# Both feed-forward blocks by column blocks with twelve of 22 up pairs each as seven half-size products, and the last four down tiles by halves of the tokens

## The chip, the cores and the metric

The kernel runs on one core of a Trainium2 chip. The metric is the device time of one execution in microseconds. TensorE (PE) multiplies, VectorE (DVE) and ScalarE (ACT) do the elementwise work, and SyncE (SP) issues the transfers between HBM and SBUF. Matrix products land in eight PSUM banks.

## The reference

A trunk of two layers on 512 tokens of width 1024, in float32. Every layer adds a token mixer and then a feed-forward block to the residual stream:

```python
for i in range(2):                       # mixer 0: gated linear attention, mixer 1: short gated convolution
    x = x + mixer_i(rmsnorm(x, norm_mix_g[i]))
    h = rmsnorm(x, norm_ffn_g[i])
    up = causal_dwconv(h @ w_up[i], conv_w[i])       # 1024 -> 2 * 2816, three taps along the tokens
    a, u = up[..., :2816], up[..., 2816:]
    x = x + (silu(a) * u) @ w_down[i]                # 2816 -> 1024
return rmsnorm(x, final_norm_g)
```

## The kernel before

Activations lie channel by token: the residual is eight tiles `x[k]` of 128 channels by 512 tokens. Every float32 operand is split into two parts of a shorter type, h and l (`halve` for weights, `split_to` and `norm_parts` for activations), and one product is three matmuls (`mm3`: wh xh, wh xl, wl xh) that accumulate in a PSUM bank. The split of a weight unit is a cast on ACT (L124) and a subtraction on DVE (L125).

`Weights` holds the order of all weight units. A raw unit is loaded by SP into one of six buffers (`wraw`), split into one of four pairs of buffers (`wsp`), and handed out by `take`, which at each call has a unit split that is used two calls later.

The feed-forward block has 22 pairs `j`: an a tile and a u tile of 128 channels. A plain pair is two `group`s of 24 matmuls (eight k, three each, 512 tokens wide). Each result is scaled by `r`, convolved (`conv3`: one ACT and two DVE operations), joined with Silu, and split into `g{j}`. A down tile `dn{m}` is a sum over the `g{j}`.

In layer 0 `ffn_blocks` goes by `BLOCKS` of 6, 5, 5 and 6 pairs: while it makes the pairs of one block it also makes the eight down tiles over the block before, one or two after each pair, and adds each to `x[m]`. The last block's eight tiles stand at the end. `SEVEN` names nine pairs that are made by Strassen's scheme: the two output tiles, the two halves of k and the two halves of the tokens form a 2 by 2 product, done as seven products of 12 matmuls, 256 tokens wide. `seven_first` does four of them (`updc`, `upab`), a down tile follows, and `seven_last` does three. Sums of weights are made on DVE by `Weights.forms` (L134 to L141), sums of activations once for each layer by `seven_forms` after pairs 1 to 4, and the results are put together by `L634` to `L651`.

In layer 1 `ffn_up` makes 22 plain pairs, and then eight down tiles follow over all 22 pairs at once (`DOWN_CUTS` cuts their weights in three). The eighth, `dn7`, is done by halves of the tokens (`last_group`, `last_square`), so that the final norm of the first half (`last_sums`, `last_rms`, `last_rows`, `last_out`) lies beside the matmuls of the second. What remains after the last matmul is the residual, square, sum, root, broadcast, scaling and output of the second half.

The order of instructions on each engine is not the program's order alone: a planner takes the program's dependencies and its own costs and places an instruction as soon as it finds it ready, earlier program lines first.

Of the kernel before, what the change touches and what calls it, by code (L numbers as in the profile page):

```python
# [15 lines left out]
P = 128  # L16
# [9 lines left out]
EPS = 1e-6  # L26
UNIT = 1024
WARM = 10
DOWN_CUTS = ((0, 8), (8, 16), (16, 22))
BLOCKS = ((0, 6), (6, 11), (11, 16), (16, 22))  # L30
SEVEN = (7, 9, 10, 12, 14, 15, 17, 19, 21)


@with_exitstack
def trunk_kernel(ctx, tc, xT, w_qk, w_v, w_g, w_up_gate, b_gate, w_go, w_sc, w_so, w_up, w_dn,
# [15 lines left out]
    def wk(name, shape=(P, T), dt=F32, bufs=2, tag=None, pool=work):  # L51
        return pool.tile(list(shape), dt, tag=tag or name, name=name, bufs=bufs)


    def tk(name, shape, bufs=2):
        return wk(name, shape, bufs=bufs, pool=tiny)

    def bt(tag, name, shape=(P, T), dt=F32):
        return big.tile(list(shape), dt, tag=tag, name=name)
# [135 lines left out]
    def ff_steps():  # L195
        steps = [("up", j) for j in range(*BLOCKS[0])]
        for b in range(1, len(BLOCKS)):
            n = BLOCKS[b][1] - BLOCKS[b][0]
            for i, j in enumerate(range(*BLOCKS[b])):
                dn = [("dn", b - 1, m) for m in range(KD * i // n, KD * (i + 1) // n)]  # L200
                steps += [("s1", j), dn[0], ("s2", j)] + dn[1:] if j in SEVEN else [("up", j)] + dn
        return steps + [("dn", len(BLOCKS) - 1, m) for m in range(KD)]

    for st in ff_steps():
        if st[0] == "dn":
            a, b = BLOCKS[st[1]]
            W.add(w_dn[0, st[2]][:, a * P:b * P])
        elif st[0] == "s1":
            pair = W.add_pair(w_up[0, 2 * st[1]], w_up[0, 2 * st[1] + 1])
        elif st[0] == "s2":  # L210
            W.end_pair(pair)
        else:
            W.add(w_up[0, 2 * st[1]])
            W.add(w_up[0, 2 * st[1] + 1])
    for src in ([w_sc[i] for i in range(3 * KD)] + [w_so[i] for i in range(KD)]
                + [w_up[1, j] for j in range(2 * NFF)]
                + [w_dn[1, m][:, a * P:b * P] for m in range(KD) for a, b in DOWN_CUTS]):
        W.add(src)
    take = W.take


# [53 lines left out]
    def group(name, xs, nunits=1):  # L275
        out = ps(name)
        k = 0
        for _ in range(nunits):
            for w in take():
                mm3(out, w, xs[k], k == 0, k == len(xs) - 1)  # L280
                k += 1
        assert k == len(xs)
        return out
# [28 lines left out]
    def sum_parts(sq):  # L312
        h = wk("sh", dt=F32R, tag="sq")
        l = wk("sl", dt=F32R, tag="sq")
        S.copy(h, sq)
        V.tensor_sub(l, sq, h.bitcast(F32))
        return h, l

    def inv_rms_rows(parts, cnt):

        o = ps("sums")
        for i, a in enumerate(parts):
            PE.matmul(o, lhsT=onesr, rhs=a, start=i == 0, stop=i == 1)
        r = wk("r", bufs=2)
        S.activation(r, o, AF.Sqrt, bias=epst, scale=1.0 / cnt)  # L325
        V.reciprocal(r, r)  # L326
        return r
# [243 lines left out]
    residual(lambda m: go[m] if m < 2 else group(f"go{m}", yparts), 1)  # L571


    def ffn_up(l):
        gp, r = [], None
        for j in range(NFF):
            ups = [group("up0", xparts)]
            if j == 0:
                sums = sum_parts(acc[0])
            ups.append(group("up1", xparts))  # L580
            if j == 0:
                r = inv_rms_rows(sums, D)
            cs = []
            for i in range(2):
                u = wk("u", bufs=3)
                V.tensor_mul(u, ups[i], r)  # L586
                cs.append(conv3(u, ffcw[:, l, i * NFF + j, :], f"c{i}"))
            S.activation(cs[0], cs[0], AF.Silu)  # L588
            V.tensor_mul(cs[1], cs[1], cs[0])
            gp.append(split_to(cs[1], f"g{j}", f"b{j}"))  # L590
        return gp

    def seven_forms(k, gi, y):


        lo, hi = slice(0, HT), slice(HT, T)
        g1, g2 = col(gi, k), col(gi, k + 4)
        S.activation(y[:, lo], x[k][:, hi], AF.Copy, scale=g1)
        S.activation(y[:, hi], x[k + 4][:, hi], AF.Copy, scale=g2)
        ta, tb = wk("ta", tag="sq"), wk("tb", tag="sq")  # L600
        V.scalar_tensor_tensor(ta[:, lo], x[k][:, lo], g1, y[:, lo], op0=ALU.mult, op1=ALU.subtract)
        V.tensor_sub(tb[:, lo], y[:, lo], y[:, hi])
        V.scalar_tensor_tensor(ta[:, hi], x[k][:, lo], neg[:, k:k + 1], tb[:, lo], op0=ALU.mult, op1=ALU.add)
        V.scalar_tensor_tensor(tb[:, hi], x[k + 4][:, lo], g2, ta[:, hi], op0=ALU.mult, op1=ALU.add)
        a = split_to(ta, f"ta{k}", f"b{14 + 2 * k}")
        b = split_to(tb, f"tb{k}", f"b{15 + 2 * k}")
        return [tuple(p[:, c] for p in t) for t in (a, b) for c in (lo, hi)]
# [45 lines left out]

    def ffn_blocks(l, gi, gnext):
        gp, r, tf = {}, None, [[], [], [], []]
        V.tensor_scalar_mul(neg, vec[:, gi * KD:(gi + 1) * KD], -1.0)
        for st in ff_steps():
            if st[0] == "dn":
                _, b, m = st
                part = group(f"dn{m}", [gp[j] for j in range(*BLOCKS[b])])  # L660
                V.tensor_add(x[m], x[m], part)  # L661
                if b == len(BLOCKS) - 1:
                    norm_parts(m, gnext)
                    norm_squares(m)
                continue
            j = st[1]
            if st[0] == "s1":
                begun = seven_first(tf)
                continue
            if st[0] == "s2":  # L670
                us = seven_last(*begun, tf)
                for u in us:
                    V.tensor_mul(u, u, r)  # L673
            else:
                ups = [group("up0", xparts)]
                if j == 0:
                    sums = sum_parts(acc[0])
                ups.append(group("up1", xparts))
                if j == 0:
                    r = inv_rms_rows(sums, D)  # L680
                    y = wk("y", tag="acc", bufs=1)
                us = [wk("u", bufs=3) for _ in range(2)]
                for u, up in zip(us, ups):
                    V.tensor_mul(u, up, r)
            cs = [conv3(us[i], ffcw[:, l, i * NFF + j, :], f"c{i}") for i in range(2)]
            S.activation(cs[0], cs[0], AF.Silu)  # L686
            V.tensor_mul(cs[1], cs[1], cs[0])
            gp[j] = split_to(cs[1], f"g{j}", f"b{j % 11}")
            if len(SEVEN) and 1 <= j <= 4:
                for t, f in zip(tf, seven_forms(j - 1, gi, y)):  # L690
                    t.append(f)

    HT = T // 2
    neg = tk("neg", (P, KD), bufs=1)
    ffn_blocks(0, 1, 2)


# [18 lines left out]
    residual(lambda m: group(f"so{m}", yparts), 3)  # L716


    gp = ffn_up(1)
    for i in range(3):  # L720
        W.hold[len(W.units) - 3 + i] = lambda i=i: [
            [bt(f"x{2 * i + j}{hl}", f"wlast{i}{j}{hl}", (P, T), F32R) for hl in "hl"] for j in range(2)]
    for m in range(KD - 1):
        V.tensor_add(x[m], x[m], group(f"dn{m}", gp, nunits=3))  # L724
        norm_squares(m)
    wlast = take() + take() + take()

    def last_group(op, th, ks):
        c = slice(th * HT, (th + 1) * HT)
        for k in ks:  # L730
            gh, gl = gp[k]
            mm3(op, wlast[k], (gh[:, c], gl[:, c]), k == 0, k == NFF - 1)

    def last_square(op, th):
        c = slice(th * HT, (th + 1) * HT)
        V.tensor_add(x[KD - 1][:, c], x[KD - 1][:, c], op)
        sq = wk("sq", (P, HT))
        V.tensor_mul(sq, x[KD - 1][:, c], x[KD - 1][:, c])
        return sq

    def last_sums(pt, sq, th):
# [31 lines left out]
            V.tensor_tensor(o, o, rb.unsqueeze(1).to_broadcast([P, 2, HT]), ALU.mult)  # L773
            nc.sync.dma_start(out[a:a + 2, :, c].rearrange("a p t -> p a t"), o)

    ops = [ps("dn7a")[:, 0:HT], ps("dn7b")[:, 0:HT]]
    pts = [[ps(f"sums{th}{t}") for t in range(2)] for th in range(2)]
    last_group(ops[0], 0, range(NFF))
    last_scale(0, range(KD - 1))
    sq = last_square(ops[0], 0)  # L780
    last_scale(0, (KD - 1,))
    last_group(ops[1], 1, range(0, 5))
    last_sums(pts[0], None, 0)
    last_sums(pts[0], sq, 0)
    rl = last_rms(pts[0], 0)
    last_scale(1, range(KD - 1))
    last_group(ops[1], 1, range(5, 10))
    rb = last_rows(rl)
    last_out(rb, 0)
    last_group(ops[1], 1, range(10, NFF - 1))  # L790
    last_sums(pts[1], None, 1)
    last_group(ops[1], 1, (NFF - 1,))
    sq = last_square(ops[1], 1)
    last_scale(1, (KD - 1,))
    last_sums(pts[1], sq, 1)
    last_out(last_rows(last_rms(pts[1], 1)), 1)
# [53 lines left out]
```

## Time and profile before

| | before |
|---|---|
| time, median of 3 runs | 1111.91 us (1111.66 to 1113.05) |
| profiled execution: time / span | 1112.06 us / 1110.0 us |
| PE busy | 1100.6 us, 99% |
| DVE busy | 754.6 us, 68% |
| ACT busy | 488.9 us, 44% |
| mean granted clock of TensorE | 0.997 |

The span is from the first to the last instruction of the profiled execution. The 2.06 us beside it lie around it. Matmuls are pipelined, so one lasts longer than the distance to the next; the pace is read from the chain of work, which gives a stretch and the number of its matmuls.

### The profile page before, as it was taken

To read this page: it belongs to the slowest core of one execution; us is meant where nothing else is said; L and a number is where in the kernel's file an instruction comes from. 1 tells how busy PE (TensorE), PEld (TensorE's weight loads), DVE (VectorE), ACT (ScalarE), POOL (GpSimd) and SP (SyncE) were. 2 spreads that over 40 slices of the span, in tenths; PEclk is the share of its full clock that TensorE was granted. 3 is DMA by queue.
4 is the path that set the end of the run, shared out by engine and by line. 5 is a ranking of instruction groups with operands and counts; after the bars stand their busy time and mean duration, and the time that the engine had idled before them with its cause. 6 is when DMAs were issued, how large, how long until landed. Compare 5 with 4: busy or idle time off the path is not lost.

```text
span 1110.0 us, 13420 instructions
## 1 busy us (share of the span) xinstructions
PE 1100.6 (99%) x5344; PEld 931.3 (84%) x5344; DVE 754.6 (68%) x1019; ACT 488.9 (44%) x688; POOL 5.1 (0%) x18
## 2 busy tenths in 40 slices
PE   9999999999999999999999999999999999999997
PEld 7888888888889889888888888888888888888887
DVE  7864675599787888887866555558777777743313
ACT  6565664465344444444543222335444444432321
POOL 1000000000000000000000000000000000000000
PEclk9999999999999999999999999999999999999998
DMA  8222123323233233333332233322222233333302
GB/s 297 96 94 77 62 72 114 96 71 105 85 101 98 90 97 113 103 98 83 119 113 95 95 98 96 106 99 96 95 95 95 95 95 96 88 102 88 102 1 77
DMA packets 34338, 108.19 MB, mean 97 GB/s; under 512 B 3746, under 2 KB 6562, under 8 KB 34276
## 3 DMA queue, kind: packets, MB, share of 16 engines
q1 hardware_dynamic: 34276, 107.34, 30.2%
q8 instruction: 42, 0.69, 0.2%
q14 instruction: 20, 0.16, 0.0%
HBM read 105.23 MB, written 2.10 MB: 97 GB/s over the span
## 4 chain that ended last, share of the span: by engine, by line
PE 99%; DMA 0%; DVE 0%; ACT 0%; SPq 0%; issue 0%; DVEq 0%
PE up L273 34%; PE dn L273 20%; PE updc L614 5%; PE g L273 4%; PE v L273 4%; PE scb L273 4%; PE scu L273 4%; PE scc L273 4%; PE go L273 4%; PE so L273 4%; PE upab L614 4%; PE k L273 2%; PE q L273 2%; PE dn7b L273 1%; PE dn7a L273 1%; PE o L494 1%
## 5 line engine op out<-in xcount | busy, mean ns | idle before, releaser
L124 ACT CAST wh<-wr 128x1024 fp32r<-128x1024 f32 (+4 forms) x227 | 217.0, 957 | 356.1 <-issue 88.3
L125 DVE TENSOR_TENSOR wl<-wr,wh 128x1024 fp32r<-128x1024 f32 (+4 forms) x227 | 250.4, 1106 | 107.8 <-ACT wh L124 106.3
L273 PE MATMUL up<-xh,wh 128*128 128x512 f32 x560 | 217.9, 389 | 0.0
L273 PE MATMUL up<-xl,wh 128*128 128x512 f32 x560 | 217.9, 389 | 0.0
L273 PE MATMUL up<-xh,wl 128*128 128x512 f32 x560 | 217.8, 389 | 0.0
L273 PEld LDWEIGHTS up<-xl,wh 128*128 128x128 f32 x560 | 105.1, 188 | 21.8
L273 PEld LDWEIGHTS up<-xh,wh 128*128 128x128 f32 x560 | 105.1, 188 | 21.8
L273 PEld LDWEIGHTS up<-xh,wl 128*128 128x128 f32 x560 | 105.1, 188 | 21.6
L332 ACT ACTIVATE c<-u,ffcw 128x512 f32<-128x512 f32 x88 | 62.1, 720 | 19.2 <-DVE u L673 11.8
L334 DVE SCALAR_TENSOR_TENSOR c<-u,ffcw,c 128x510 f32<-128x510 f32 x88 | 64.9, 747 | 1.7
L333 DVE SCALAR_TENSOR_TENSOR c<-u,ffcw,c 128x511 f32<-128x511 f32 x88 | 64.7, 746 | 1.2 <-ACT c L332 0.6
L586 DVE TENSOR_TENSOR u<-up,r 128x512 f32<-128x512 f32 x44 | 30.1, 688 | 37.7 <-PE up L273 37.6
L588 ACT ACTIVATE c<-c 128x512 f32<-128x512 f32 x22 | 13.9, 632 | 41.5 <-DVE c L334 41.4
L661 DVE TENSOR_TENSOR x<-x,dn 128x512 f32<-128x512 f32 x32 | 21.9, 684 | 13.8 <-PE dn L273 13.5
L326 DVE RECIPROCAL r<-r 128x512 f32<-128x512 f32 x8 | 26.8, 3352 | 6.3 <-ACT r L325 6.3
L309 ACT ACTIVATE sq<-x 128x512 f32<-128x512 f32 x34 | 21.0, 623 | 19.0 <-DVE x L724 17.8
L686 ACT ACTIVATE c<-c 128x512 f32<-128x512 f32 x22 | 13.9, 631 | 26.6 <-DVE c L334 26.5
L273 PE MATMUL g<-xh,wh 128*128 128x512 f32 x64 | 25.6, 400 | 0.0
L273 PE MATMUL v<-wh,xh 128*128 128x512 f32 x64 | 25.3, 395 | 0.0
L273 PE MATMUL g<-xh,wl 128*128 128x512 f32 x64 | 24.9, 390 | 0.0
L273 PE MATMUL v<-wh,xl 128*128 128x512 f32 x64 | 24.9, 390 | 0.0
L273 PE MATMUL v<-wl,xh 128*128 128x512 f32 x64 | 24.9, 389 | 0.0
(924 smaller groups left out, 2384.8 us busy)
## 6 DMA issues: line engine op xcount, KB each, us to landing
wr<-in_w_up SPq DMA_DIRECT2D x88, 512.0 KB, 3.4
wr<-in_w_sc SPq DMA_DIRECT2D x24, 512.0 KB, 3.4
wr<-in_w_dn SPq DMA_DIRECT2D x24, 384.0 KB, 3.1
wr<-in_w_dn SPq DMA_DIRECT2D x16, 512.0 KB, 3.5
wr<-in_w_dn SPq DMA_DIRECT2D x16, 320.0 KB, 2.9
wr<-in_w_v SPq DMA_DIRECT2D x8, 512.0 KB, 3.6
wr<-in_w_g SPq DMA_DIRECT2D x8, 512.0 KB, 3.5
wr<-in_w_go SPq DMA_DIRECT2D x8, 512.0 KB, 3.4
```

The lines of the kernel that those rows point to most:

```text
L124: S.copy(hh, src)
L125: V.tensor_sub(ll, src, hh.bitcast(F32))
L273: PE.matmul(out, lhsT=a, rhs=b, start=first and i == 0, stop=last and i == 2)
L309: S.activation(sq, x[k], AF.Square)
L326: V.reciprocal(r, r)
L332: S.activation(c, u, AF.Copy, scale=cw[:, 2:3])
L333: V.scalar_tensor_tensor(c[:, 1:], u[:, :T - 1], cw[:, 1:2], c[:, 1:], op0=ALU.mult, op1=ALU.add)
L334: V.scalar_tensor_tensor(c[:, 2:], u[:, :T - 2], cw[:, 0:1], c[:, 2:], op0=ALU.mult, op1=ALU.add)
L586: V.tensor_mul(u, ups[i], r)
L588: S.activation(cs[0], cs[0], AF.Silu)
L614: PE.matmul(out, lhsT=a, rhs=b, start=first and k == 0 and i == 0, stop=k == 3 and i == 2, skip_group_check=not first)
L661: V.tensor_add(x[m], x[m], part)
```

## The change

Layer 1's feed-forward block goes through `ffn_blocks` too, so `ffn_up` and `DOWN_CUTS` go away. `SEVEN` holds twelve pairs in place of nine, for both layers. In layer 1 the last block's down tiles 0 to 3 are made whole and 4 to 7 (`HALVED = 4`) first for the first half of the tokens and then for the second, with the four weight units held in the `wsp` buffers.

```diff
-SEVEN = (7, 9, 10, 12, 14, 15, 17, 19, 21)
+HALVED = 4
+SEVEN = (7, 8, 9, 10, 12, 13, 14, 15, 17, 18, 20, 21)
...
+    add_ffn(0)
+    for src in [w_sc[i] for i in range(3 * KD)] + [w_so[i] for i in range(KD)]:
         W.add(src)
+    add_ffn(1)
...
     def ffn_blocks(l, gi, gnext):
         gp, r, tf = {}, None, [[], [], [], []]
+        neg = tk("neg", (P, KD), bufs=1)
         V.tensor_scalar_mul(neg, vec[:, gi * KD:(gi + 1) * KD], -1.0)
         for st in ff_steps():
             if st[0] == "dn":
                 _, b, m = st
+                if gnext is None and b == len(BLOCKS) - 1 and m == HALVED:
+                    break
                 part = group(f"dn{m}", [gp[j] for j in range(*BLOCKS[b])])
                 V.tensor_add(x[m], x[m], part)
                 if b == len(BLOCKS) - 1:
-                    norm_parts(m, gnext)
+                    if gnext is not None:
+                        norm_parts(m, gnext)
                     norm_squares(m)
                 continue
...
-    gp = ffn_up(1)
...
-    for m in range(KD - 1):
-        V.tensor_add(x[m], x[m], group(f"dn{m}", gp, nunits=3))
-        norm_squares(m)
-    wlast = take() + take() + take()
+    gp = ffn_blocks(1, 3, None)
+    wlast = {m: take() for m in range(HALVED, KD)}
...
+        if m == KD - 1:
+            V.tensor_mul(sq, x[m][:, c], x[m][:, c])
+        else:
+            S.activation(sq, x[m][:, c], AF.Square)
+            V.tensor_add(acc[0][:, c], acc[0][:, c], sq)
...
-    last_group(ops[0], 0, range(NFF))
...
+    last_scale(0, range(HALVED))
+    for m in range(HALVED, KD):
+        ops[m] = ps(f"dnl{m}")
+        last_group(m, 0)
+        sq = last_square(m, 0)
+    last_scale(0, range(HALVED, KD))
+    last_group(HALVED, 1)
+    last_square(HALVED, 1)
     last_sums(pts[0], None, 0)
     last_sums(pts[0], sq, 0)
     rl = last_rms(pts[0], 0)
+    last_scale(1, range(HALVED))
+    last_group(HALVED + 1, 1)
+    last_square(HALVED + 1, 1)
     rb = last_rows(rl)
+    last_group(HALVED + 2, 1)
+    last_square(HALVED + 2, 1)
     last_out(rb, 0)
+    last_scale(1, range(HALVED, KD - 1))
+    last_group(KD - 1, 1, range(len(gp) - 1))
     last_sums(pts[1], None, 1)
+    last_group(KD - 1, 1, range(len(gp) - 1, len(gp)))
+    sq = last_square(KD - 1, 1)
     last_scale(1, (KD - 1,))
     last_sums(pts[1], sq, 1)
     last_out(last_rows(last_rms(pts[1], 1)), 1)
```

## Rows read from the trace of the kernel before

**Rows 1.** The page's busy times: engine, us (share of the span), instructions.
```profile
PE 1100.6 (99%) x5344; PEld 931.3 (84%) x5344; DVE 754.6 (68%) x1019; ACT 488.9 (44%) x688; POOL 5.1 (0%) x18
```

**Rows 2.** Waits of PE over the whole span: us in total, times, longest.
```profile
PE warm L75 <- DVE warm L63: 1.5, 1, 1.5
PE sums L744 <- DVE sq L738: 1.0, 1, 1.0
```

**Rows 3.** The chain that ended last, in order of time: start, us, what, matmuls.
```profile
310.06 10.88 PE up L273 x48
320.94 4.08 PE dn L273 x18
325.02 2.87 PE updc L614 x24
327.89 2.88 PE upab L614 x24
...
334.88 2.87 PE updc L614 x24
337.75 1.44 PE upab L614 x12
...
372.46 3.40 PE dn L273 x15
...
437.47 3.43 PE dn L273 x15
...
527.67 36.35 PE dn L273 x159
...
978.37 104.72 PE dn L273 x462
```

**Rows 4.** Busy time by stretch: layer 0's four blocks of pairs, in order.
```profile
222.42:276.82 54.40, 54.40 (x241) 45.06 (x241) 54.28 (x81) 34.00 (x51) 0.00 (x0) 1.00 0.28 90
276.82:361.58 84.76, 84.76 (x493) 75.27 (x493) 67.69 (x102) 36.26 (x56) 0.00 (x0) 1.00 0.32 97
361.58:440.90 79.32, 79.32 (x469) 70.77 (x469) 66.75 (x102) 35.56 (x56) 0.00 (x0) 1.00 0.33 99
440.90:527.67 86.77, 86.77 (x502) 76.96 (x502) 69.65 (x104) 38.93 (x60) 0.00 (x0) 1.00 0.32 94
```

**Rows 5.** DVE in order of time, 390 to 402 us: start, us, instruction.
```profile
390.03 0.83 DVE L125 TENSOR_TENSOR wl<-wr,wh 128x640 fp32r<-128x640 f32 x1 [2.22 <-ACT wh L124]
390.77 0.42 DVE L649 TENSOR_TENSOR u<-updc,u 128x256 f32<-128x256 f32 x1
391.11 0.42 DVE L650 TENSOR_TENSOR u<-e,u 128x256 f32<-128x256 f32 x1
...
398.97 0.68 DVE L134 TENSOR_TENSOR s<-wr,wr 128x512 f32<-128x512 f32 x1
399.57 1.22 DVE L125 TENSOR_TENSOR wl<-wr,wh 128x1024 fp32r<-128x1024 f32 x1
400.71 0.68 DVE L289 TENSOR_TENSOR g12l<-c,g12h 128x512 fp32r<-128x512 f32 x1
401.31 0.74 DVE L333 SCALAR_TENSOR_TENSOR c<-u,ffcw,c 128x511 f32<-128x511 f32 x1
401.97 0.68 DVE L140 TENSOR_TENSOR wr<-wr,wr 128x512 f32<-128x512 f32 x1
```

**Rows 6.** Waits of DVE from 276.8 to 564 us: us in total, times, longest.
```profile
DVE wl L125 <- ACT wh L124: 31.5, 27, 3.5
DVE x L661 <- PE dn L273: 12.8, 13, 1.9
DVE s L134 <- DMA wr<-in_w_up: 3.5, 4, 1.2
```

**Rows 7.** DVE in order of time: the last 640-wide split for the second block.
```profile
429.64 0.82 DVE L125 TENSOR_TENSOR wl<-wr,wh 128x640 fp32r<-128x640 f32 x1
```

**Rows 8.** DVE in order of time, at the end of the run.
```profile
1096.32 2.48 DVE L773 TENSOR_TENSOR o<-o,rb 128x512 f32<-128x512 f32 x4 [2.24 <-PE rb L757]
1100.72 0.42 DVE L736 TENSOR_TENSOR x<-x,dn7b 128x256 f32<-128x256 f32 x1 [1.91 <-PE dn7b L273]
```

More of the change, by code (lines that the diff above doesn't have):

```diff
@@ L28 @@
 WARM = 10
-DOWN_CUTS = ((0, 8), (8, 16), (16, 22))
 BLOCKS = ((0, 6), (6, 11), (11, 16), (16, 22))
-SEVEN = (7, 9, 10, 12, 14, 15, 17, 19, 21)
+HALVED = 4
+SEVEN = (7, 8, 9, 10, 12, 13, 14, 15, 17, 18, 20, 21)
 @with_exitstack
@@ L202, in ff_steps, with add_ffn @@
         return steps + [("dn", len(BLOCKS) - 1, m) for m in range(KD)]
[L204 to L217, printed above, removed]
+    def add_ffn(l):
+        for st in ff_steps():
+            if st[0] == "dn":
+                a, b = BLOCKS[st[1]]
+                W.add(w_dn[l, st[2]][:, a * P:b * P])
+            elif st[0] == "s1":
+                pair = W.add_pair(w_up[l, 2 * st[1]], w_up[l, 2 * st[1] + 1])
+            elif st[0] == "s2":
+                W.end_pair(pair)
+            else:
+                W.add(w_up[l, 2 * st[1]])
+                W.add(w_up[l, 2 * st[1] + 1])
+    add_ffn(0)
+    for src in [w_sc[i] for i in range(3 * KD)] + [w_so[i] for i in range(KD)]:
         W.add(src)
+    add_ffn(1)
     take = W.take
@@ L571, in trunk_kernel, with seven_forms @@
     residual(lambda m: go[m] if m < 2 else group(f"go{m}", yparts), 1)
[L574 to L593, printed above, removed]
+    def seven_forms(k, gi, y, neg):
         lo, hi = slice(0, HT), slice(HT, T)
@@ L689, in ffn_blocks @@
             if len(SEVEN) and 1 <= j <= 4:
-                for t, f in zip(tf, seven_forms(j - 1, gi, y)):
+                for t, f in zip(tf, seven_forms(j - 1, gi, y, neg)):
                     t.append(f)
+        return [gp[j] for j in range(*BLOCKS[-1])]
     HT = T // 2
-    neg = tk("neg", (P, KD), bufs=1)
     ffn_blocks(0, 1, 2)
@@ L716, in trunk_kernel, with last_group @@
     residual(lambda m: group(f"so{m}", yparts), 3)
-    gp = ffn_up(1)
-    for i in range(3):
-        W.hold[len(W.units) - 3 + i] = lambda i=i: [
-            [bt(f"x{2 * i + j}{hl}", f"wlast{i}{j}{hl}", (P, T), F32R) for hl in "hl"] for j in range(2)]
-    for m in range(KD - 1):
-        V.tensor_add(x[m], x[m], group(f"dn{m}", gp, nunits=3))
-        norm_squares(m)
-    wlast = take() + take() + take()
-    def last_group(op, th, ks):
+    gp = ffn_blocks(1, 3, None)
+    wlast = {m: take() for m in range(HALVED, KD)}
+    def last_group(m, th, ks=range(len(gp))):
         c = slice(th * HT, (th + 1) * HT)
@@ L731, in last_group, with last_square @@
             gh, gl = gp[k]
-            mm3(op, wlast[k], (gh[:, c], gl[:, c]), k == 0, k == NFF - 1)
-    def last_square(op, th):
+            mm3(ops[m][:, c], wlast[m][k], (gh[:, c], gl[:, c]), k == 0, k == len(gp) - 1)
+    def last_square(m, th):
         c = slice(th * HT, (th + 1) * HT)
-        V.tensor_add(x[KD - 1][:, c], x[KD - 1][:, c], op)
+        V.tensor_add(x[m][:, c], x[m][:, c], ops[m][:, c])
         sq = wk("sq", (P, HT))
-        V.tensor_mul(sq, x[KD - 1][:, c], x[KD - 1][:, c])
+        if m == KD - 1:
+            V.tensor_mul(sq, x[m][:, c], x[m][:, c])
+        else:
+            S.activation(sq, x[m][:, c], AF.Square)
+            V.tensor_add(acc[0][:, c], acc[0][:, c], sq)
         return sq
@@ L774, in last_out @@
             nc.sync.dma_start(out[a:a + 2, :, c].rearrange("a p t -> p a t"), o)
-    ops = [ps("dn7a")[:, 0:HT], ps("dn7b")[:, 0:HT]]
     pts = [[ps(f"sums{th}{t}") for t in range(2)] for th in range(2)]
-    last_group(ops[0], 0, range(NFF))
[L779 to L782, printed above, removed]
+    ops = {}
+    last_scale(0, range(HALVED))
[6 more added lines that the diff above has]
+    last_square(HALVED, 1)
     last_sums(pts[0], None, 0)
@@ L785, in trunk_kernel @@
     rl = last_rms(pts[0], 0)
-    last_scale(1, range(KD - 1))
-    last_group(ops[1], 1, range(5, 10))
+    last_scale(1, range(HALVED))
+    last_group(HALVED + 1, 1)
+    last_square(HALVED + 1, 1)
     rb = last_rows(rl)
+    last_group(HALVED + 2, 1)
+    last_square(HALVED + 2, 1)
     last_out(rb, 0)
-    last_group(ops[1], 1, range(10, NFF - 1))
+    last_scale(1, range(HALVED, KD - 1))
+    last_group(KD - 1, 1, range(len(gp) - 1))
     last_sums(pts[1], None, 1)
-    last_group(ops[1], 1, (NFF - 1,))
-    sq = last_square(ops[1], 1)
+    last_group(KD - 1, 1, range(len(gp) - 1, len(gp)))
+    sq = last_square(KD - 1, 1)
     last_scale(1, (KD - 1,))
```

## The prediction

> **What bounds the kernel now.** I read the busy times first, then what PE waits for, then the chain of work in order of time, and last the busy time by stretch and the order on DVE. PE is busy 99% of the span [rows 1], and the longest two of its four waits are 1.5 us at the start and 1.0 us at the end [rows 2]. So until the last matmul the time is the number of matmuls times their pace, and the chain gives that pace [rows 3]: a plain pair is 48 matmuls of 512 tokens in 10.88 us, 0.2267 us each; twelve matmuls of 256 tokens are 1.44 us and 24 are 2.87, 0.1196 each. That is 5% more than half of 0.2267: a half-size matmul is not quite half as long. The reader should see two things there: what a pair costs in either form, and that nothing lies between the pieces. DVE, at 68% over the span, is the engine that could take PE's place. In the four stretches of layer 0's pairs it is busy 54.28 of 54.40, 67.69 of 84.76, 66.75 of 79.32 and 69.65 of 86.77 us [rows 4], where three pairs of each of the last three stretches are half-size.
>
> **PE, pairs.** A half-size pair is 2.87 + 2.88 + 2.87 + 1.44 = 10.06 us. A down tile of 15 matmuls takes 3.40 us behind a plain pair and 3.43 behind half-size products [rows 3]; each half-size pair has two such changes back to full width, so it costs 10.12 us. Against 10.88 it saves 0.76 us. Layer 0 gets three more of them and layer 1 twelve: 15 x 0.76 = 11.4 us off PE.
>
> The Trainium skill ("TensorE: Matmul & The Clock Gate", section "Back-to-back issue gap") gives the distance between matmuls at full clock as columns / 2.4 ns plus 2.5 ns, an estimate of 109 ns for 256 columns and 216 for 512. By it a pair would go from 48 x 0.2158 = 10.36 to 84 x 0.1092 = 9.17 us, and 15 pairs would save 17.8 us. The trace differs (119.6 and 226.7 ns for these very instructions), and my sum goes by the trace.
>
> **PE, down tiles of layer 1.** Before: seven tiles of 66 matmuls, 462 in 104.72 us, and 132 of half width. After: three blocks give (6 + 5 + 5) x 3 x 8 = 384, the last block's first four tiles 72, so 456 of full width, and 4 x 2 x 18 = 144 of half width. That is 6 x 0.2267 = 1.36 us less and 12 x 0.1196 = 1.44 us more: +0.1 us.
>
> **The joint before the last block's tiles.** In layer 0 pair 21 is half-size and its g21 is late for the eight tiles behind it: 159 matmuls take 36.35 us [rows 3], against 159 x 0.2267 = 36.04. In layer 1 the down tiles now show no such loss (462 in 104.72 is the bare pace). It gets the same joint: +0.3 us. Between 0 and, if pair 20 just ahead (plain before, half-size now) makes g21 later in both layers, 1.5.
>
> **DVE.** Its distances from one start to the next, back to back [rows 5]: 0.60 us for 512 elements, 1.14 for a split of 1024, 0.74 for one of 640, 0.66 for a tap of the convolution, 0.34 for a half tile out of PSUM (0.36 taken, as some stand a little apart). A plain pair is two splits of 1024, four operations of 512 and four taps: 7.3 us. A half-size pair has four sums of weights and three half splits (7 x 0.60), two splits of 1024, five half tiles, and the same four and four: 4.2 + 2.3 + 1.8 + 2.4 + 2.6 = 13.3 us. A down tile of a block of five is a split and an addition to x, 1.34 us; of a block of six about 1.47, by the line between 640 and 1024. The check: three half-size pairs, two plain ones and eight tiles make 39.9 + 14.6 + 10.7 = 65.2, where the third stretch shows 66.75, so I add 2%.
>
> After the change the second stretch holds four half-size pairs, one plain and eight tiles of six: 73.7 us of 84.0 that PE needs. The third: 72.6 of 78.6. The fourth, with its eighth tile: 80.1 of 89.4. DVE is at 88, 92 and 90%, so by the sum it still fits beside PE in both layers. The 24 further additions to x in layer 1 are in these sums. It is tight inside a stretch: a half-size pair with one tile of five needs 14.9 us of DVE in 13.5 us of PE, 1.4 short (pairs 13, 17, 20), and pair 8 with one tile of six is 0.9 short; pairs with two tiles have 0.6 to over 1 us of room, plain pairs over 5. What covers the shortfall is the lead with which DVE works. The last 640-wide split of the third stretch ends at 430.46 [rows 7] and PE begins that tile at 437.47 [rows 3]: 7.0 us early. A lag of 1.4 us that the next pairs pay back should not reach PE. If it does, this is the cost named below. I take 0.5 us for all of it, between 0 and some 42.
>
> The first stretch of layer 1 gains the sums of activations (`seven_forms`). Layer 0's stretch has the same pairs with the same sums, and there DVE is busy 54.28 of 54.40 us with PE at its bare pace [rows 4]; part of that is work done ahead. Nothing is added for it; uncovered, it would delay the pairs 6 and 7 behind it.
>
> **Loads.** SP's order changes to that of layer 0, with two raw units for each half-size pair; the bytes are the same. DVE stood 3.5 us for such loads in four waits, 1.2 at most [rows 6]. With a third more pairs that is about 4.7 us for each layer, on DVE and under the lead of 7.0: nothing on PE.
>
> **The tail.** The four held units fill all four split buffers, so ACT's cast for tile 7 waits until the matmuls of tile 3 end, with the squares and scalings queued behind it; PE needs it 54 half-width matmuls later (6.5 us), the cast and split take about 2. Nothing. Before, the four output scalings of the first half (2.48 us) start at 1096.32 and are done 1.9 us before the last residual add at 1100.72 [rows 8]. Now their row broadcast comes ahead of tile 6's second half, and the program has them behind tile 6's square. If the planner puts them where they are ready, they run beside the 18 matmuls of tile 6 (2.15 us) and delay its add by 0.3. If it keeps the program's order, they start some 1.3 us after tile 6 (three operations like the 0.42 us add) and end at 3.8, while tile 7's matmuls end at about 2.4: 1.4 us later at the end. I take 0.3, since in layer 0 the joint showed matmuls taken out of the program's order when others were not ready. What follows the last matmul is the same chain as before.
>
> **Sum.** -11.4 + 0.1 + 0.3 + 0.5 + 0.3 = -10.2 us. The profiled execution took 1112.06, so 1101.9; the median of the runs stands 0.15 below it: **1101.7 us**, 0.9% faster. With nothing lost anywhere it would be 1100.6.
>
> **Rivals.**
> - *DVE's idle time does not shrink* (slower). DVE idles 17.1, 12.6 and 17.1 us in the second to fourth stretch [rows 4], mostly at the head of its queue for a cast (31.5 us) or a load [rows 6]. If that stayed when the work grows, the stretches would grow by 73.7 + 17.1 - 84.0 = 6.8, 6.6 and 7.8 us, 21 us a layer, and the time would be about 1111.9 - 11.3 + 42 = 1143. It decides from 27% of this on (11.3 of 42). The Trainium skill (the same page, section "Architectural detail: the array is 16× 32×32, not 1× 128×128") says that the queues of ScalarE and VectorE are strictly first in, first out; the trace agrees (2.22 us of idle time before one split, until its cast came [rows 5]). Against it: the casts wait for buffers that PE frees, so DVE stands there because it is early, with 7.0 us in hand; a late DVE does not meet these waits.
> - *The short pairs each stop PE* (no change). If no lead carries over from pair to pair, pairs 13, 17 and 20 cost 1.4 each and pair 8 0.9: 5.1 a layer, 10.2 in all, and the time is about 1111. For it: 92% in the third stretch leaves little. Against it: the lead, and that pairs 17 and 19 have one tile each now and PE has no wait there.
> - *The new pairs run at the distances 215.8 and 109.2 ns* (faster still). 1111.9 - 17.8 and the losses above give about 1095. The rows on the same lines of code are against it.
>
> **Chances.** Forecast 0.84 (its own range 1100 to 1105, with the dearer tail and joint), idle time that stays 0.08, short pairs 0.06, the faster pace 0.02. Less than 0.2% (2.2 us) can't be told from no change here. Faster by more: 0.88, the forecast, the fast pace and part of the short pairs; within it 0.05; slower 0.07. The range from 1099.9 to 1106.5 leaves out most of the rivals and holds the bounds of tail and joint.
>
> **What would show it.** In the chain: half-size pairs of 10.06 us in both layers, 24 in all, with down tiles between them and no piece for DVE, ACT or a load among them; in the stretches: DVE near 90% and PE at 100%; at the joints before the last tiles: under 1 us above the bare pace; at the end: the four scalings done before the last residual add. The forecast is wrong if PE waits for splits or for g tiles inside the stretches, or if the half-size matmuls come slower than 0.1196 us where four such pairs follow each other.

## The result and the profile after

The changed kernel takes **1099.84 us** (median of 4 runs, 1099.70 to 1099.97) where the kernel before takes 1111.94 (1111.66 to 1113.05): a ratio of 0.9889, 95% interval 0.9872 to 0.9906, 12.1 us faster. The profiled execution has a span of 1098.0 us against 1110.0. The forecast was 1101.7 with a range from 1099.9 to 1106.5: the direction and the main saving held, but the gain is 1.9 us larger than forecast, and the time lies 0.06 us below the range. In the rounds of the experiments the kernel before took 1111.43 to 1111.62 us (medians); against these the gain is 11.6 to 11.8 us.

The page's busy times of the changed kernel, the answer to [rows 1]:

```profile
PE 1088.0 (99%) x5890; PEld 946.5 (86%) x5890; DVE 859.1 (78%) x1259; ACT 533.2 (49%) x802; POOL 5.1 (0%) x18
```

DVE has 104.5 us more work, PE 12.6 less, and PE is still the engine that sets the time. Its waits are few and short and lie at either end, as in [rows 2] (one of 0.6 us at the start is new); between the first and the last pair it has none. The chain of the changed kernel in order of time (start, us, what, matmuls), the answer to [rows 3]; first layer 0, then the end of layer 1:

```profile
319.71 2.87 PE updc L597 x24
322.58 1.44 PE upab L597 x12
324.02 2.88 PE updc L597 x24
326.90 2.88 PE upab L597 x24
329.78 4.11 PE dn L275 x18
...
525.10 36.27 PE dn L275 x159
...
1050.13 19.95 PE dn L275 x87
1070.08 10.79 PE dnl L275 x90
1080.88 0.79 PE sums L730 x8
1081.66 2.73 PE dnl L275 x22
1084.40 0.45 PE rb L743 x4
1084.84 3.85 PE dnl L275 x32
1088.69 0.02 issue
1088.71 0.43 DVE x L718
```

The half-size products keep their pace (24 in 2.87 us), also where one such pair follows another without a down tile between, as at 324.02: there the change back to full width falls away. The last three stretches are those of pairs 6 to 21, down to the last half-size product. Layer 0's end at 525.10 where they ended at 527.67, 2.36 us shorter once the start is taken out (250.85 to 248.49); layer 1's last three stretches take 248.49 us too, where 16 plain pairs and the same tiles would take 257.72. That is 0.77 us a pair.

The busy times by stretch of the changed kernel, layer 1's second to fourth (stretch, its length, busy times of PE, PEld, DVE, ACT and POOL with the number of instructions, granted clock, DMA share, GB/s, as in [rows 4]; layer 0's three agree with them within 0.2 us of DVE):

```profile
801.64:885.62 83.98, 83.98 (x529) 76.34 (x529) 72.83 (x113) 38.69 (x62) 0.00 (x0) 1.00 0.32 97
885.62:964.16 78.54, 78.54 (x505) 71.83 (x505) 72.17 (x114) 38.18 (x62) 0.00 (x0) 1.00 0.33 101
964.16:1053.53 89.37, 89.37 (x553) 80.81 (x553) 77.37 (x122) 42.33 (x68) 0.00 (x0) 1.00 0.31 91
```

PE fills every one. DVE's 73.7, 72.6 and 80.1 us of the forecast came out as 72.8, 72.2 and 77.4 (a part of the last pair's work lies behind the fourth stretch). Its idle time fell from 17.1, 12.6 and 17.1 us to 11.2, 6.4 and 12.0. The waits of DVE in layer 0 of the changed kernel, 276.61 to 561.37 us (total, times, longest), against [rows 6]:

```profile
DVE wl L125 <- ACT wh L124: 26.1, 24, 2.8
DVE x L647 <- PE dn L275: 5.5, 7, 1.2
DVE s L134 <- DMA wr<-in_w_up: 0.3, 1, 0.3
```

With a third more half-size pairs DVE waits less for casts, for PE and for loads: a busier engine comes later to each of these, when more of them are done.

Last, DVE at the end of the changed kernel, in order of time (start, us, instruction), the answer to [rows 8]:

```profile
1084.88 0.69 DVE L759 TENSOR_TENSOR o<-o,rb 128x512 f32<-128x512 f32 x1 [0.50 <-PE rb L743]
1085.48 0.42 DVE L724 TENSOR_TENSOR acc<-acc,sq 128x256 f32<-128x256 f32 x1
1085.82 1.28 DVE L759 TENSOR_TENSOR o<-o,rb 128x512 f32<-128x512 f32 x2
1087.02 0.41 DVE L718 TENSOR_TENSOR x<-x,dnl 128x256 f32<-128x256 f32 x1
1087.35 0.68 DVE L759 TENSOR_TENSOR o<-o,rb 128x512 f32<-128x512 f32 x1
1087.97 0.43 DVE L724 TENSOR_TENSOR acc<-acc,sq 128x256 f32<-128x256 f32 x1
1088.71 0.42 DVE L718 TENSOR_TENSOR x<-x,dnl 128x256 f32<-128x256 f32 x1 [0.32 <-PE dnl L275]
```

The four scalings (`o<-o,rb`) run as soon as the row broadcast is there and around the residual add of tile 6 (1087.02), and the last residual add still starts 0.02 us behind the last matmul. And the row sums of the tiles before, which stood 0.34 us long ahead of the last three matmuls in the kernel before, now come behind them, beside that add:

```profile
1088.39 0.28 PE L275 MATMUL dnl<-g21h,wl 128*128 128x256 f32 x1
1088.51 0.55 PE L730 MATMUL sums<-ones,acc 128*128 128x1 f32 x4
1089.65 0.49 PE L730 MATMUL sums<-ones,sq 128*128 128x1 f32 x3 [0.59 <-DVE sq L721]
```

Behind the last matmul 9.31 us follow in both profiled executions, but not by the same pieces. The last row broadcast took 1.24 us in the execution of the kernel before, at a granted clock of 0.50, and 0.72 us in the changed kernel, at 1.00. In the run with the pairs of layer 0 alone, whose end is that of the kernel before, it took 0.72 us too. The two lines are from the chains of the kernel before and of that run:

```profile
1102.81 1.24 PE rb L757 x4
1100.58 0.72 PE rb L757 x4
```

In that run 8.83 us follow the last matmul. So some 0.5 us of the 12.0 between the two spans is the clock in one execution of the kernel before, and the changed kernel's end is some 0.5 us longer: from its last scaling to the end of the span it takes 3.96 us, against 3.45 and 3.49. Why, no run here shows.

### The profile page after: what moved, and what is told of

The parts are those of the page before. It is cut to its first block, busy times and chain, and to the rows that moved or that the text cites. A ratio compares the mean times of both kernels' runs of the same rounds, so it can differ in the third digit from the quotient of the medians.

```text
span 1098.0 us, 14911 instructions
## 1 busy us (share of the span) xinstructions
PE 1088.0 (99%) x5890; PEld 946.5 (86%) x5890; DVE 859.1 (78%) x1259; ACT 533.2 (49%) x802; POOL 5.1 (0%) x18
## 4 chain that ended last, share of the span: by engine, by line
PE 98%; DMA 0%; DVE 0%; ACT 0%; SPq 0%; issue 0%; DVEq 0%
PE dn L275 20%; PE up L275 20%; PE updc L597 13%; PE upab L597 9%; PE g L275 4%; PE v L275 4%; PE so L275 4%; PE scb L275 4%; PE scu L275 4%; PE scc L275 4%; PE go L275 4%; PE k L275 2%; PE q L275 2%; PE dnl L275 2%; PE o L496 1%; PE o L498 0%
## 5 line engine op out<-in xcount | busy, mean ns | idle before, releaser
L275 PE MATMUL up<-xh,wh 128*128 128x512 f32 x320 | 124.5, 389 | 0.0
L275 PE MATMUL up<-xl,wh 128*128 128x512 f32 x320 | 124.5, 389 | 0.0
L275 PE MATMUL up<-xh,wl 128*128 128x512 f32 x320 | 124.5, 389 | 0.0
L275 PEld LDWEIGHTS up<-xh,wh 128*128 128x128 f32 x320 | 60.1, 188 | 12.5
L275 PEld LDWEIGHTS up<-xh,wl 128*128 128x128 f32 x320 | 60.1, 188 | 12.5
L275 PEld LDWEIGHTS up<-xl,wh 128*128 128x128 f32 x320 | 60.1, 188 | 12.4
L597 PE MATMUL upab<-xh,wh 128*128 128x256 f32 x192 | 54.3, 283 | 0.0
L597 PE MATMUL upab<-xl,wh 128*128 128x256 f32 x192 | 54.3, 283 | 0.0
L597 PE MATMUL upab<-xh,wl 128*128 128x256 f32 x192 | 54.3, 283 | 0.0
L647 DVE TENSOR_TENSOR x<-x,dn 128x512 f32<-128x512 f32 x60 | 40.9, 682 | 11.4 <-PE dn L275 11.0
L597 PEld LDWEIGHTS upab<-xh,wh 128*128 128x128 f32 x192 | 36.9, 192 | 0.0
```

What stands on the lines that cost most here:

```text
L275: PE.matmul(out, lhsT=a, rhs=b, start=first and i == 0, stop=last and i == 2)
L597: PE.matmul(out, lhsT=a, rhs=b, start=first and k == 0 and i == 0, stop=k == 3 and i == 2, skip_group_check=not first)
```

## The experiments

The theory at this point: nearly the whole gain is PE's, 0.77 us for each of 15 pairs, and DVE costs nothing as long as its sum over a few stretches stays under PE's. The rivals are those of the prediction (DVE's idle time stays; short pairs stop PE one by one), and that layer 1's new order or the halves carry part of the gain.

**The pairs of layer 0 alone.** The kernel before with only the list of pairs changed:

```diff
-SEVEN = (7, 9, 10, 12, 14, 15, 17, 19, 21)
+SEVEN = (7, 8, 9, 10, 12, 13, 14, 15, 17, 18, 20, 21)
```

> The kernel before with the twelve half-size pairs in layer 0 alone; layer 1 as before. If the gain is the matmuls' own (0.77 us a pair, 15 pairs), three more pairs give 2.4 us: about 1109.5, and the rest of the 12.1 us belongs to layer 1. If the gain came from layer 1's new order of the down tiles, or from the tail, rather than from the pairs, layer 0's share would still be 2.4, and the pairs of layer 1 have to be told apart by another run; if the gain is not by pairs at all, this run shows well under 2.

Measured: 1109.25 us, ratio 0.9981 (0.9971 to 0.9990), 2.2 us faster than the 1111.43 of the kernel before beside it. Layer 0 has its share by its three pairs, and the 9.4 us from here to the changed kernel belong to layer 1.

**Layer 1 by blocks and halves, without half-size pairs.**

```diff
-    def ff_steps():
+    def ff_steps(l):
...
-                steps += [("s1", j), dn[0], ("s2", j)] + dn[1:] if j in SEVEN else [("up", j)] + dn
+                steps += [("s1", j), dn[0], ("s2", j)] + dn[1:] if l == 0 and j in SEVEN else [("up", j)] + dn
...
-            if len(SEVEN) and 1 <= j <= 4:
+            if l == 0 and 1 <= j <= 4:
```

> The changed kernel with twelve half-size pairs in layer 0 and none in layer 1, whose down tiles still go by blocks and whose last four still go by halves. If the pairs carry the gain, it is 12 x 0.77 = 9.2 us slower than the changed kernel, within 0.5 us of the run with the twelve pairs in layer 0 alone (1109.2): the new order of the down tiles and the halves bring nothing by themselves. If the order or the halves brought a part, it is faster than that run by this part.

Measured: 1109.27 us (0.9979, 0.9969 to 0.9989), level with the run above. The order of the down tiles and the halves bring nothing by themselves; the twelve pairs of layer 1 are the 9.4 us between this run and the changed kernel.

**More work on DVE.** In the program of each half-size pair of the changed kernel, additions whose result nobody reads (three, then six). Their operands are there all along, so the planner need not keep them at their pair:

```diff
                 us = seven_last(*begun, tf)
+                for _ in range(3):
+                    V.tensor_add(wk("sq"), xparts[0][0].bitcast(F32), xparts[0][1].bitcast(F32))
```

> The changed kernel with three further additions of 512 elements on DVE in each half-size pair (1.8 us; their result is not used). DVE's sums become about 80.2 of 84.0, 79.4 of 78.5 and 84.6 of 89.4 us in the three stretches of a layer. Theory (DVE costs nothing until its sum passes PE's, and the lead covers small excesses): at most 1 to 2 us slower than the changed kernel, 1099.8 to 1102. Rival that DVE's idle time does not shrink: 24 x 1.8 = 43 us slower. Rival that no lead carries over: the eight pairs with one tile cost 1.8 us each and the others most of 1.2, 20 to 30 us slower.

Measured: 1100.19 us (0.9898, 0.9883 to 0.9913), 0.35 us above the changed kernel (0.1 us between the profiled spans). DVE's idle time that does not shrink would have cost 43 us: that rival is out. The trace has 20 of a layer's 36 additions in the second stretch, 12 in the third and 4 in the fourth, where the program has 12 in each. So the price for each short pair, 20 to 30 us here, is not met either, but the additions did not lie pair by pair; the runs with 15 and 16 pairs below test that rival with work that belongs to its pair. Layer 1's second and third stretch:

```profile
801.75:885.73 83.98, 83.98 (x530) 76.34 (x529) 82.98 (x132) 38.68 (x62) 0.00 (x0) 1.00 0.31 93
885.73:964.27 78.54, 78.54 (x506) 71.83 (x505) 77.88 (x125) 38.16 (x63) 0.00 (x0) 1.00 0.34 105
```

DVE is busy 99% of both, and PE still has no gap. The first of them shows more than the 80.2 us summed for it, since the planner pulled eight further additions ahead into it; in the fourth DVE is busy 79.9 of 89.3 us where 84.6 was summed.

> The same with six further additions (3.6 us) in each half-size pair: 87.4 of 84.0, 86.6 of 78.5 and 91.8 of 89.4 us. Theory: DVE is the bound in all three stretches, 3.4 + 8.1 + 2.4 = 14 us a layer less what the lead of 7 us takes up once, so 14 to 28 us slower than the changed kernel, 1114 to 1128, and PE waits for splits and evictions. Idle time that does not shrink: 86 us slower.

Measured: 1121.99 us (1.0091, 1.0076 to 1.0106), 22 us above the changed kernel, inside the 14 to 28 that the sum gave and far from 86. Here each stretch has 24 of the additions. Now DVE is the bound, and the waits of PE show where. Waits of PE in that run, 360 to 1100 us (total, times, longest):

```profile
PE dn L275 <- ACT wh L124: 6.5, 2, 3.3
PE upab L597 <- DVE wl L125: 3.6, 2, 1.8
PE dn L275 <- ACT g21h L290: 2.5, 2, 1.3
```

PE waits for casts and splits of weights and for g21, the waits that the prediction named as the sign of being wrong. The room runs out between 36 and 72 further additions a layer, 1.8 and 3.6 us for each pair on the mean. The waits sum to some 13 of the 20.8 us between the profiled spans. A further part are matmuls at a lower clock behind such a wait. Six additions, the whole third stretch of layer 0, then the time around one wait of 3.25 us in it:

```profile
360.62:447.22 86.60, 81.16 (x506) 73.10 (x505) 84.04 (x136) 39.11 (x62) 0.00 (x0) 0.98 0.29 90
432.00:434.60 2.60, 0.00 (x0) 0.00 (x0) 2.60 (x5) 2.26 (x4) 0.00 (x0) 1.00 0.00 0
434.60:437.00 2.40, 2.34 (x6) 1.85 (x7) 2.40 (x5) 0.96 (x2) 0.00 (x0) 0.52 0.40 103
437.00:439.00 2.00, 2.00 (x8) 1.65 (x7) 2.00 (x3) 0.00 (x0) 0.00 (x0) 0.73 0.87 284
439.00:441.00 2.00, 2.00 (x16) 1.84 (x15) 1.15 (x3) 1.05 (x1) 0.00 (x0) 1.00 0.91 255
```

The stretch is 8.1 us longer than in the changed kernel (78.54 us): 5.4 of them PE stood, and 2.6 are matmuls that took longer. After the wait the granted clock is 0.52, near the 1.2 GHz level. The chain goes through the additions, and it gives the down tile behind the wait 5.26 us for its 15 matmuls where 3.43 is the pace: 1.8 us on top of the wait.

```profile
423.11 3.01 DVE sq L660 x5
434.66 5.26 PE dn L275 x15
```

**Fifteen and sixteen pairs.** All pairs of the last two blocks, then all of the last three:

```diff
-SEVEN = (7, 8, 9, 10, 12, 13, 14, 15, 17, 18, 20, 21)
+SEVEN = (7, 8, 9, 10, 11, 12, 13, 14, 15, 16, 17, 18, 19, 20, 21)
...
+SEVEN = (6, 7, 8, 9, 10, 11, 12, 13, 14, 15, 16, 17, 18, 19, 20, 21)
```

> The changed kernel with 15 half-size pairs in each layer (7 to 21). PE alone would save 6 x 0.77 = 4.6 us more: 1095.2. DVE's sum in the stretch of the third block is then about 78.3 us of 77.8 and in the fourth about 89.4 of 87.8, so it is over PE by 0.5 and 1.6 us in each layer. Theory (a sum over PE costs only what the lead of 7 us cannot cover): 1095 to 1097. Rival (each pair with a single down tile stops PE by its own shortfall of 1.4 us): 6 more such pairs would take their gain back and more, 1099 to 1103.

Measured: 1095.53 us (0.9858, 0.9841 to 0.9874).

> The changed kernel with all 16 pairs of the last three blocks (6 to 21) half-size in both layers: the most that the scheme allows here. PE saves 8 x 0.78 = 6.2 us against the changed kernel, so 1093.6 if nothing is lost. The run with 15 pairs kept DVE at 96 to 98% of the last two stretches with PE at its bare pace; here the second stretch gets its fifth pair too and DVE's sum there is about 81 of 82.5 us. Theory (only a sum over PE's costs): 1093.5 to 1095. Rival (short pairs stop PE where no plain pair is left to catch up): no faster than the run with 15, 1095.5 or more.

Measured: 1093.33 us (0.9834, 0.9820 to 0.9849). The version with 16 pairs beats both kernels: it is 18.1 us faster than the kernel before and 6.5 us faster than the changed one. Each further pair pays its 0.77 to 0.80 us: from the first pair of layer 0 to the last block's down tiles it is 314.22 us with 12 pairs, 311.90 with 15 and 311.10 with 16. These are the chain's lines there, with 15 and with 16 pairs (first pairs at 211.07 and 210.85):

```profile
522.97 36.25 PE dn L275 x159
521.95 36.07 PE dn L275 x159
```

The 2.0 us between these two spans are 0.8 in each layer, 0.2 at the start and 0.2 in these last tiles. In neither run does a wait of PE stand between the first and the last pair, so no pair with one tile stops it. The three stretches of layer 0 with 16 pairs:

```profile
276.00:358.00 82.00, 82.00 (x560) 76.44 (x559) 79.73 (x129) 41.49 (x67) 0.00 (x0) 1.00 0.33 106
358.00:434.00 76.00, 76.00 (x534) 71.43 (x534) 72.96 (x119) 40.05 (x66) 0.00 (x0) 1.00 0.33 100
434.00:521.00 87.00, 87.00 (x620) 82.11 (x619) 85.92 (x143) 46.79 (x77) 0.00 (x0) 1.00 0.33 94
```

DVE at 97, 96 and 99% beside a PE without a gap.

**Two tiles by halves in place of four.**

```diff
-HALVED = 4
+HALVED = 6
...
-    last_scale(1, range(HALVED))
-    last_group(HALVED + 1, 1)
-    last_square(HALVED + 1, 1)
+    last_scale(1, range(KD - 1))
     rb = last_rows(rl)
-    last_group(HALVED + 2, 1)
-    last_square(HALVED + 2, 1)
     last_out(rb, 0)
-    last_scale(1, range(HALVED, KD - 1))
```

> The changed kernel with two of the last down tiles by halves in place of four. PE saves 2 x (36 x 0.1199 - 18 x 0.2267) = 0.5 us of half-width matmuls. The row sums, root, broadcast and four scalings of the first half (0.8 + 0.9 + 0.45 + 2.5 = 4.6 us) then lie beside the 18 matmuls of one tile and the sums (3.4 us) instead of beside two tiles more. If the scalings can be placed around the last additions, 0.5 us faster than the changed kernel; if they hold up the last residual add, up to 1.2 us less the 0.5, so 0.7 slower.

Measured: 1100.30 us (0.9899, 0.9882 to 0.9915), 0.5 above the changed kernel, 0.4 in the spans. From the chain of this run behind its last matmul:

```profile
1087.76 0.43 DVE x L718
1088.21 0.42 DVE sq L721
1088.64 2.39 DVE o L759 x4
1091.03 0.09 DVE rl L737
```

The last matmul comes 1.0 us earlier than in the changed kernel, but all four scalings of the first half now stand between the last square and the root of the second. Two tiles more in halves hide them: that is what the halves of four tiles pay for, some 0.4 us.

**The row sums ahead of the last matmuls.**

```diff
-    last_sums(pts[1], None, 1)
-    last_group(KD - 1, 1, range(len(gp) - 1, len(gp)))
+    summed = last_sums(pts[1], None, 1)
+    with tc.issue_after(summed.ins):
+        last_group(KD - 1, 1, range(len(gp) - 1, len(gp)))
```

(`last_sums` returns its last matmul for this.)

> The changed kernel with the last three matmuls of tile 7 kept behind the row sums of the residual's squares, as the program has them (in the changed kernel the planner issues these row sums after the last matmul, beside the residual add). The square of tile 6 is added at 1088.40 in the changed kernel's profile, 0.3 us before its last matmul ends, so the row sums cannot start before that, and 0.34 us of sums and 0.47 us of three matmuls follow: the last matmul ends at about 1089.2 in place of 1088.7. If the moved sums saved the 0.3 us that the total shows, this run is 0.3 to 0.6 us slower than the changed kernel; if they lay on no path, it is within 0.1.

Measured: 1100.96 us (0.9907, 0.9889 to 0.9923), 1.1 above the changed kernel; 1.3 in the spans, of which 0.3 are a later start of layer 0 (211.22 against 210.88). From the chain of this run:

```profile
1088.39 0.39 DVE acc L724
1088.82 0.61 PE sums L730 x4
1089.43 0.48 PE dnl L275 x3
```

In this order PE waits for the square of tile 6, which stands behind the scalings on DVE. From the joint (the first matmul behind the last half-size product) to the last matmul it costs 0.9 us, more than the 0.3 to 0.6 expected. The prediction had feared the scalings for the last residual add, not for these sums. The planner's order has neither this wait nor the sums ahead of the last matmuls.

## Where the prediction was right, and which terms of its sum failed

The sum term by term, in the spans of the two profiled executions:

| term | forecast, us | measured, us | from |
|---|---|---|---|
| 15 pairs | -11.4 | -11.6 | 250.85 - 248.49 = 2.36 and 257.72 - 248.49 = 9.23 |
| layer 1's down tiles | +0.1 | 0.0 | -6 x 0.2267, and 17.37 for 144 against 16.02 for 132 |
| joints | +0.3 | +0.15 | 36.27 against 36.35; 19.95 against 87 x 0.2267 = 19.72 |
| DVE late | +0.5 | 0.0 | no wait of PE in the stretches |
| tail | +0.3 | -0.3 | row sums and broadcast ahead of PE's last matmul 1.24 against 1.57; then 9.31 in both |
| start | 0 | -0.2 | first pair at 210.88 against 211.09 |
| sum | -10.2 | -12.0 | spans |

What failed are the two loss terms, "DVE late" and "tail": 0.8 us charged, -0.3 measured. They are 1.1 of the 1.8 us between the sums, and the range left only 0.7 us for gains beyond the pairs.

- **What bounds it, and the pairs:** right. A pair saves 0.77 us, at the pace read from the chain, in both layers. The size is short by 0.2 because the forecast charged each pair with two changes of width; four pairs in each layer are followed directly by another and have one.
- **The faster pace of the third rival** did not come: the new pairs run at 119.6 to 119.9 ns a matmul like the old. The Trainium skill ("TensorE: Matmul & The Clock Gate", section "Back-to-back issue gap"), which calls its formula the gap of an isolated matmul, gives 109 ns for 256 columns by it, an estimate that the trace does not bear out.
- **DVE:** the sums were right within 1 us in two stretches, and so was the conclusion that they fit. The 0.5 us for a lag that reaches PE was charged without a row that showed one, and measured 0.0. In the run with three further additions, 36 of them a layer (0.60 us each, 21.6 us) reach PE with under 0.4 us in all; the run with six shows that DVE becomes the bound where its sum is clearly over PE's.
- **The slower rival** (idle time stays) fails on the measured idle time, which shrank by 5 to 6 us in each stretch. The short pairs' rival fails on the changed kernel's own stretches, where PE has no wait, and on 15 and 16 pairs.
- **The tail:** the prediction asked only whether the scalings delay the last add, and gave 0.3 us for it. They do not, and the planner also took the row sums from ahead of the last three matmuls: -0.3 us. "What follows the last matmul is the same chain as before" does not hold: the equal 9.31 us are luck, a broadcast of 1.24 us in the profiled kernel before against an end that is 0.5 us longer in the changed one. Beside the run with layer 0 alone (8.83 us) the tail would be +0.15, by other pieces than the forecast's.
- **The base:** the forecast starts from the 1112.06 us of that one execution. From the 1111.43 us of the later runs the same sum gives 1101.2, and the measured time is still 1.4 us below it.
- **The floor of the range:** "With nothing lost anywhere it would be 1100.6" allowed 0.7 us for a gain beyond the pairs. The terms that went the other way (0.2 pairs, 0.1 tiles, 0.3 tail, 0.2 start) sum to 0.8, the joints give 0.15 back, and the time beside the span, in no term, fell by 0.3 (from 2.06 to 1.73 in the profiled executions). The start differs between executions (210.81 to 211.30 in those profiled here), so its 0.2 us is not the change's. A time 0.06 us below the range is less than the 0.27 us between the changed kernel's own executions.

What stays open: why the last outputs end later, and how the planner would place 17 or more pairs, since the first block has no down tiles to go between the products; it was not tried.

## What to carry to other kernels

Where one engine runs without a gap, the saving is the work taken from it at its measured pace. Here a second engine could be filled to 96% and more of a stretch without cost: its idle time, which was waiting for casts, loads and the first engine, shrank as the work grew. Find the room by adding useless work to the second engine until the first one waits, and look in the trace where that work was placed; here there was room for 16 pairs and another 6.5 us. In the last few microseconds count not only what may be late but also what can move behind the last instruction of the bound engine, and compare more than one execution: here a broadcast of 0.72 us took 1.24 in one of them.

## What the runs showed that was not expected

With 16 pairs DVE was busy 96 to 99% of stretches of 76 to 87 us, its operations tied to casts on ACT, loads or products, and PE had no gap there. A wait of PE of 3.25 us cost more than itself: the granted clock behind it was 0.52 over 2.4 us and 0.73 over the next 2.0, and eight matmuls stood 0.36 to 0.60 us apart in place of 0.2267.
